# Two-layer hybrid block on one core: when the gathers are queued, and where the expert tables are zeroed

## The chip, the cores and the metric

One core of one Trainium2 chip. The metric is device microseconds of one execution of the whole program. A core has five engines that run their own instruction streams in order: PE (matmul, with its weight loads listed as PEld), DVE, ACT, POOL and SP. SP only issues DMAs here, and POOL issues the indirect ones. All DMAs share 16 DMA engines.

## The reference, cut to what matters

Two layers. Each has adaLN and RMSNorm, one input projection, three kinds of attention, an output projection, and then product-key expert retrieval (PEER), whose last step is what the change touches. There are 512 latent and 256 context tokens (six tiles of 128); layer 1 needs only the four latent tiles.

```python
def peer(h, wq, subkeys, u, v):
    q = (h @ wq).astype(jnp.float32).reshape(t, PEER_HEADS, 2, PEER_KDIM // 2)
    s = jnp.einsum('thpd,hpnd->thpn', q, subkeys.astype(jnp.float32))
    s_top, i_top = lax.top_k(s, PEER_TOPK)
    ...
    best, pos = lax.top_k(cand, PEER_TOPK)
    expert = jnp.take_along_axis(cand_idx, pos, axis=-1)
    gate = jax.nn.softmax(best, axis=-1)
    ...
        a = jax.nn.gelu(jnp.einsum('cd,chkd->chk', hc, u[ec]).astype(jnp.float32), approximate=False)
        w = (gc * a).astype(v.dtype)
        return jnp.einsum('chk,chkd->cd', w, v[ec])
```

Each token picks 8 heads x 16 = 128 of 16384 experts; `u` and `v` are 16384 x 1024 per layer.

## The kernel before, in words

**Dense experts.** The kernel does not gather `v`. It streams all of `v` (128 steps of 128 experts, 512 KB each, L1126) and multiplies it on PE with a matrix of weights per token tile, mostly zeros (`vpass`, L1141). It does this for groups of tiles: (2,3,4) and then (5,0,1) in layer 0, (2,3) and then (1,0) in layer 1. Each 512 KB block of `v` is split into two float16 parts, the high one on ACT (L1127) and the low one on DVE (L1128); PE needs both.

**Activations.** For most tiles ("dense": 2, 3, 4, 5 in layer 0; 2, 3, 1 in layer 1) the product with `u` is also dense: `upass` streams `u` in two halves of 64 steps (L1034, L1054; low parts of the splits on DVE, L144, but on POOL for the first 24 steps, L154), and spills the gelu of it to memory. For the others ("picked": 0 and 1 in layer 0; 0 in layer 1) `gather` fetches the picked rows of `u`: per tile 128 indirect DMAs of 128 rows, 512 KB each, issued by POOL (L946) into a ring of three buffers `r`; DVE multiplies each with the tile's own rows `hg` and sums (L952). That sum goes into the tile `a`, of which there is one buffer, so the second picked tile cannot write it until the first one's values have left.

**Tables.** The weights of a tile other than 2 and 3 go through a table of 8 MB in device memory. `Table.clear` zeroes it (eight pieces of 1 MB by SP, L1257). `Table.put` scatters the values with 128 indirect DMAs per tile, issued by POOL (L1266): for dense tiles the gates (`gs`), for picked tiles the finished weights (`a`). `Table.get` reads it back for `vpass` (L1282). The first group of layer 0 needs table 4, the second one tables 5, 0 and 1; `need` emits what is missing before a group begins.

**What sets the order.** The program is emitted by generators in three lists: `rg` (modulation, routing, picks), `bg` (attention, later the gathers), `sq` (puts). `tick(list, rate)` advances a list by so many items per step of `upass` or `vpass`; the rates per half pass are `RATES` for `bg` and `SRATES` for `sq`. A scheduler then orders the instructions of each engine. `queue_behind` gives a gather or a put an order-only tie behind the latest split `lo_ins`; no engine waits for it on the chip. `zg` holds the clears, ticked in `project` once `ch > 3` and flushed at its end. `routing` and `pick` run beside the first half of `upass`; a pick ends with the indices `ix` and `to` (L913) and 128 short DVE instructions `gjk` (L921). The indices of the picked tiles come last.

The zero tile in `mixers` (L286, L287) is allocated per layer in the pool `nqkv`, filled by POOL, and has no other tie.

Of the kernel before, what the change touches and what calls it, by code (L numbers as in the profile page):

```python
# [8 lines left out]
F32 = mybir.dt.float32  # L9
# [20 lines left out]
BIG = -3.0e38  # L30
ROPE_SCALE = {("d", "q"): 32.0 ** -0.5, ("d", "k"): 1.0, ("r", "q"): 1.0, ("r", "k"): 0.125}
RATE_NA, RATE_DF = 2.7, 1.4
RATES = {0: (0.8, 1.0, 1.5, 1.5, 0.0, 0.0), 1: (0.6, 1.2, 0.4, 0.8, 0.0, 0.0)}
SRATES = {0: (2.0, 2.9, 1.6, 1.8, 4.0, 4.0), 1: (1.5, 1.8, 0.9, 1.2, 4.0, 4.0)}
RRATE = (1.3, 1.05)
AHEAD = 2
GST = 2
# [4 lines left out]
ZC = 2048  # L42
# [5 lines left out]
class Hybrid:  # L48
# [22 lines left out]
    def consts(self):  # L71
        nc, c, tmp = self.nc, self.cst, self.tmp
        dl = tmp.tile([128, 128], F32, name="dl")
        nc.gpsimd.iota(dl, pattern=[[1, 128]], base=0, channel_multiplier=-1,
                       allow_small_or_imprecise_dtypes=True)
        io = tmp.tile([128, 128], F32, name="io")
        nc.gpsimd.iota(io, pattern=[[1, 128]], base=0, channel_multiplier=0,
                       allow_small_or_imprecise_dtypes=True)
        self.idf = c.tile([128, 128], F32, name="idf")
        nc.vector.tensor_scalar(self.idf, dl, 0.0, None, op0=OP.is_equal)  # L80
        self.idh = c.tile([128, 128], F16, name="idh")
        nc.vector.tensor_scalar(self.idh, dl, 0.0, None, op0=OP.is_equal)
        self.iox = c.tile([128, 128], F16, name="iox")
        nc.vector.tensor_copy(self.iox, io)
        self.tok = c.tile([128, 1], F32, name="tok")
        nc.gpsimd.iota(self.tok, pattern=[[0, 1]], base=0, channel_multiplier=1, allow_small_or_imprecise_dtypes=True)
        self.mhalf = c.tile([128, 8], F32, name="mhalf")
        nc.vector.memset(self.mhalf, -0.5)
        self.bcol = c.tile([128, 12, KC], F32, name="bcol")
        nc.gpsimd.dma_start(self.bcol, self.i["b_ada"])  # L90
        self.modT, self.g1, self.g2 = {}, {}, {}
        for l in range(2):
            self.modT[l] = [c.tile([128, KC, 2], F32, name=f"mod{l}_{m}") for m in range(6)]
            for nm, st in (("g1col", self.g1), ("g2col", self.g2)):
                st[l] = c.tile([128, KC], F32, name=f"{nm}{l}")
                nc.gpsimd.dma_start(st[l], self.i[nm][l])
# [173 lines left out]
    def mixers(self, l, last, wes):  # L270
# [11 lines left out]
        with ExitStack() as e:  # L282
            nap = self.pool(e, "nqkv")
            self.naT = nap.tile([128, 4, 2, T], F16, name="naT")
            self.nav = [nap.tile([128, 2, 2, 256], F16, name=f"nav{p}") for p in range(3)]
            self.zero = nap.tile([128, ZC // 4], F32, name="zero")  # L286
            self.nc.gpsimd.memset(self.zero, 0.0)  # L287
            hp = self.pool(e, "hT", 3)
            pp = self.pool(e, "prj", 2)
            ps = self.pool(e, "pps", 2, space=PSUM)  # L290
# [1 line left out]
            if l == 0:  # L292
                spare = lambda t: self.hp2.tile([128, D], F32, name=f"h2T{t}")
                vec = [self.srow(spare(x), x) for x in range(2)]
                n = iter("hl" * 99)
# [68 lines left out]
    def project(self, l, last, hp, pool, ps, ap_, att_es, xs):  # L364
        nc = self.nc
        wv = self.i["w_in"][l].rearrange("(k p) n -> p k n", p=128)

        def load(ch):
            res = []
            for k in range(0, KC, 2):  # L370
# [1 line left out]
                nc.sync.dma_start(w, wv[:, k:k + 2, ch * 256:ch * 256 + 256])  # L372
                h = pool.tile([128, 2, 256], F16, name="wh", bufs=6)
                lo = pool.tile([128, 2, 256], F16, name="wl", bufs=6)
                self.wsplit(h, lo, w)
                res += [(h[:, x], lo[:, x]) for x in range(2)]
            return res

# [645 lines left out]
    def upass(self, l, half, ps, tag, rrate, more=None):  # L1024
        nc = self.nc
# [17 lines left out]
        for jj in range(64):  # L1043
# [22 lines left out]
            if jj % 2:  # L1066
                next(steps, None)
            self.tick(self.rg, rrate)
            self.tick(self.bg, RATES[l][half])
            self.tick(self.sq, SRATES[l][half])  # L1070
        self.drain(steps)

# [161 lines left out]
class Table:  # L1234
# [19 lines left out]
    def clear(self):  # L1254
        o = self.o
        for c in range(0, 128 * 128, ZC):
            self.before.append(o.nc.sync.dma_start(self.view()[:, c:c + ZC].rearrange("i (r n) -> i r n", r=4),  # L1257
                                                  o.zero[:, None].to_broadcast([128, 4, ZC // 4])))
            yield

    def put(self, h, to, values, c, step):
# [93 lines left out]
```

## Time and profile before

| | |
|---|---|
| three runs | 4929.35 us median (4927.22 to 4931.84) |
| profiled execution | 4932.08 us, span 4930.0 us |
| PE, DVE, ACT, POOL busy | 84%, 69%, 40%, 38% |
| mean granted TensorE clock | 0.921 |
| DMA | 971.54 MB, mean 197 GB/s |
| gathers (L946), puts (L1266) | 384, 768 |
| zero pieces (L1257) | 48 of 1 MB |

The stages that the text speaks of lie so: layer 0 projects and attends until about 360 us; retention and the output projection until about 600 us; the first half of `upass` with the routing until about 1190 us; the second half until about 1612 us; the first group of `vpass` until about 2405 us; the second group until about 2920 us. Layer 1 repeats this: projections from about 2945 to 3250 us, `upass` until about 4195 us, `vpass` to the end. Busy time tells how long an engine had an instruction in work; an engine that stands still because its next instruction waits shows as idle, with the name of what ended the wait.

### The profile page before, as it was taken

The numbers are of one execution on the slowest core, as the hardware profiler recorded it, in microseconds if no ns is written. First come the engines' busy times: TensorE is split into PE (matmuls) and PEld (weight loads), VectorE is DVE, ScalarE is ACT, GpSimd is POOL, SyncE is SP. The second block draws the span as 40 slices with busy tenths as digits, with TensorE's granted clock in tenths as the row PEclk, the third lists the DMA queues.
The fourth block names the chain that finished last, engine by engine and source line by source line (L and its number), as shares of the span: only waits on it lengthen the run. The fifth ranks groups of instructions, "written<-read, shape, count | busy, mean of one in ns | idle before, by whom it ended". The sixth has DMA issues, their size and how long they took to land. (4 is left out here: it accounts for less than half of the span.)

```text
span 4930.0 us, 74817 instructions
## 1 busy us (share of the span) xinstructions
PE 4154.8 (84%) x27326; PEld 2287.3 (46%) x27326; DVE 3391.1 (69%) x7913; ACT 1981.4 (40%) x3236; POOL 1877.5 (38%) x1536
## 2 busy tenths in 40 slices
PE   4987888987898889567599999978879888999998
PEld 3664453753444334222244447745546445444443
DVE  7677559889555776566466554574698867987665
ACT  4556353432222334112233336564525322554444
POOL 4224214303777774567500002251213577761000
PEclk8997898998999989878799999978989999999999
DMA  7831343324667887977778863114446678777887
GB/s 250 298 127 35 131 124 100 111 75 129 196 207 214 256 263 224 337 262 262 228 252 269 259 219 102 50 42 135 125 127 190 214 255 267 264 259 253 265 270 238
DMA packets 512322, 971.54 MB, mean 197 GB/s; under 512 B 73824, under 2 KB 295488, under 8 KB 511952
## 3 DMA queue, kind: packets, MB, share of 16 engines
q1 hardware_dynamic: 422464, 759.66, 48.0%
q0 software_dynamic: 80032, 201.86, 12.8%
q10 hardware_dynamic: 9456, 5.24, 0.4%
q8 instruction: 214, 3.51, 0.3%
q14 instruction: 156, 1.28, 0.1%
HBM read 861.77 MB, written 104.78 MB: 196 GB/s over the span
## 5 line engine op out<-in xcount | busy, mean ns | idle before, releaser
L1141 PE MATMUL acc<-hl,gst 128*128 128x512 f16 x7680 | 1761.7, 391 | 231.2 <-ACT gst L140 151.7
L1141 PEld LDWEIGHTS <-gst 128*128 128x128 f16 x7680 | 760.8, 100 | 1201.4 <-issue 179.6
L1054 PEld LDWEIGHTS <-hl 128*128 128x128 f16 x6144 | 613.3, 101 | 726.4 <-DVE hl L144 128.7
L1127 ACT ACTIVATE hl<-s 128x1024 f16<-128x1024 f32 x512 | 538.4, 1053 | 748.0 <-PE acc L1141 393.9
L952 DVE SCALAR_TENSOR_TENSOR r<-r,hg 128x1024 f32<-128x1024 f32 x384 | 468.7, 1224 | 458.1 <-DMA r<-peer_u,ix 457.1
L946 POOL DMA_INDIRECT r<-peer_u,ix x384 | 481.8, 1255 | 665.6 <-DVE r L952 240.0
L1128 DVE TENSOR_TENSOR hl<-s,hl 128x1024 f16<-128x1024 f32 x512 | 625.4, 1222 | 140.8 <-ACT hl L1127 138.7
L1054 PE MATMUL pw<-h2Uh,hl 128*128 128x512 f16 (+1 forms) x2048 | 601.9, 371 | 83.4 <-DVE hl L144 71.0
L1054 PE MATMUL pa<-h2Uh,hl 128*128 128x512 f16 (+1 forms) x2048 | 584.2, 363 | 49.7 <-DVE hl L144 49.4
L1266 POOL DMA_INDIRECT table<-a,to x384 | 494.0, 1286 | 172.4 <-issue 122.3
L1266 POOL DMA_INDIRECT table<-gs,to x384 | 470.1, 1224 | 201.9 <-issue 128.8
L161 POOL TENSOR_TENSOR rstd<-rstd,mhalf 128x1 f32<-128x1 f32 x26 | 14.6, 562 | 1117.2 <-DVE rstd L160 1114.5
L1054 PE MATMUL pw<-h2Ul,hl 128*128 128x512 f16 (+1 forms) x1024 | 379.2, 370 | 0.0
L1054 PE MATMUL pa<-h2Ul,hl 128*128 128x512 f16 (+1 forms) x1024 | 371.7, 363 | 0.0
L169 PE MATMUL pj<-wh,hTl 128*128 128x256 f16 x1072 | 295.8, 276 | 3.0 <-DVE hTl L142 2.5
L167 PE MATMUL pj<-wh,hTh 128*128 128x256 f16 x1072 | 295.8, 276 | 1.2 <-ACT hTh L140 1.2
L168 PE MATMUL pj<-wl,hTh 128*128 128x256 f16 x1072 | 296.0, 276 | 0.0
L144 DVE SCALAR_TENSOR_TENSOR hl<-s,hl 128x1024 f16<-128x1024 f32 x208 | 255.8, 1231 | 19.2 <-ACT hl L140 19.1
L1061 ACT ACTIVATE gst<-pa 128x512 f32<-128x512 f32 (+1 forms) x128 | 69.5, 543 | 486.2 <-PE pa L1054 383.7
L154 POOL TENSOR_TENSOR wl<-wst,wh 128x512 f16<-128x512 f32 x96 | 125.3, 1319 | 287.7 <-ACT wh L153 248.8
L140 ACT ACTIVATE hl<-s 128x1024 f16<-128x1024 f32 x208 | 219.1, 1053 | 11.8 <-DMA s<-ut 10.7
L154 POOL TENSOR_TENSOR hl<-s,hl 128x1024 f16<-128x1024 f32 x48 | 106.3, 2218 | 290.0 <-ACT hl L153 264.5
(292 smaller groups left out, 7000.5 us busy)
## 6 DMA issues: line engine op xcount, KB each, us to landing
s<-peer_v SPq DMA_DIRECT2D x512, 512.0 KB, 4.6
s<-ut SPq DMA_DIRECT2D x256, 512.0 KB, 4.3
table<-zero SPq DMA_DIRECT2D x48, 1024.0 KB, 7.7
wq<-peer_wq SPq DMA_DIRECT2D x128, 256.0 KB, 3.7
spill<-gst SPq DMA_DIRECT2D x112, 256.0 KB, 4.5
wst<-w_in SPq DMA_DIRECT2D x96, 256.0 KB, 3.1
h2Ul<-table SPq DMA_DIRECT2D x192, 128.0 KB, 3.5
h2Uh<-table SPq DMA_DIRECT2D x192, 128.0 KB, 3.4
```

Of the source, the lines that this page charges most:

```text
L144: return nc.vector.scalar_tensor_tensor(lo, src, scale, hi, op0=OP.mult, op1=OP.subtract)
L154: return (lo_eng or nc.gpsimd).tensor_tensor(lo, w, hi, op=OP.subtract)
L167: nc.tensor.matmul(out, ah, bh, start=start, stop=False)
L168: nc.tensor.matmul(out, ah, bl, start=False, stop=False)
L169: nc.tensor.matmul(out, al, bh, start=False, stop=stop)
L946: self.queue_behind(nc.gpsimd.indirect_dma_start(out=r, out_offset=None, in_=self.i["peer_u"], in_offset=bass.IndirectOffsetOnAxis(ap=ix[: ...
L952: nc.vector.scalar_tensor_tensor(r, r, 1.0, h, op0=OP.mult, op1=OP.mult, accum_out=a[:, d // 16, d % 16:d % 16 + 1])
L1054: nc.tensor.matmul(pa[:, c:d], uh[:, x, k], h[:, k, c:d], start=k == 0 and i == 0, stop=k == KC - 1 and i == 2)
L1127: nc.scalar.activation(vh[:, 0], v, AF.Copy)
L1128: self.lo_ins = nc.vector.tensor_tensor(vh[:, 1], v, vh[:, 0], op=OP.subtract)
L1141: nc.tensor.matmul(acc[s][hf], pr[:, w, s, j % 2], vh[:, x, hf * 512:hf * 512 + 512], start=j == 0 and i == 0, stop=j == 127 and i == 2)
L1266: ins = o.nc.gpsimd.indirect_dma_start(out=self.d, out_offset=bass.IndirectOffsetOnAxis(ap=to[:, k, h:h + 1], axis=0), in_=values[:, c + s ...
```

## The change

Three edits in `upass`, `Table.clear`/`project` and the two tables of rates:

```diff
-RATES = {0: (0.8, 1.0, 1.5, 1.5, 0.0, 0.0), 1: (0.6, 1.2, 0.4, 0.8, 0.0, 0.0)}
-SRATES = {0: (2.0, 2.9, 1.6, 1.8, 4.0, 4.0), 1: (1.5, 1.8, 0.9, 1.2, 4.0, 4.0)}
+RATES = {0: (1.0, 1.4, 1.4, 1.4, 0.0, 0.0), 1: (1.0, 1.2, 0.5, 0.9, 0.0, 0.0)}
+SRATES = {0: (3.0, 2.6, 1.6, 1.8, 4.0, 4.0), 1: (2.5, 1.8, 0.9, 1.2, 4.0, 4.0)}
...
+        self.zero = c.tile([128, ZC // 16], F32, name="zero")
+        nc.gpsimd.memset(self.zero, 0.0)
...
-            self.zero = nap.tile([128, ZC // 4], F32, name="zero")
-            self.nc.gpsimd.memset(self.zero, 0.0)
...
-                self.wsplit(h, lo, w)
+                self.lo_ins = self.wsplit(h, lo, w)
...
-            self.tick(self.bg, RATES[l][half])
+            self.tick(self.bg, 0 if self.rg else RATES[l][half])
...
-            self.before.append(o.nc.sync.dma_start(self.view()[:, c:c + ZC].rearrange("i (r n) -> i r n", r=4),
-                                                  o.zero[:, None].to_broadcast([128, 4, ZC // 4])))
+            ins = o.nc.sync.dma_start(self.view()[:, c:c + ZC].rearrange("i (r n) -> i r n", r=16),
+                                      o.zero[:, None].to_broadcast([128, 16, ZC // 16]))
+            o.queue_behind(ins)
+            self.before.append(ins)
```

A piece of zeros is still 1 MB, now read from 512 B of each partition (16 repeats) in place of 2 KB (4 repeats), and tied behind the newest split of a `w_in` block. The zero tile is filled once, at the start. `upass` hands out no gather while `rg` holds routing or picks.

**POOL, end of the first half of `upass` in layer 0.** Before (`table_4` is tile 4's table, `r<-peer_u,ix` a gather):

```order
L154 TENSOR_TENSOR hl<-s_9374,hl 128x1024
L1266 DMA table_4_102<-gs,to 2097152x1 x68
L946 DMA r<-peer_u,ix 128x1024
L1266 DMA table_4_102<-gs,to 2097152x1 x2
L946 DMA r<-peer_u,ix 128x1024
L1266 DMA table_4_102<-gs,to 2097152x1 x2
L946 DMA r<-peer_u,ix 128x1024
L1266 DMA table_4_102<-gs,to 2097152x1 x4
```

And now (line numbers of this part are two higher):

```order
L156 TENSOR_TENSOR hl<-s_9374,hl 128x1024
L1268 DMA table_4_104<-gs,to 2097152x1 x128
L1268 DMA table_5_105<-gs,to 2097152x1 x5
L946 DMA r<-peer_u,ix 128x1024 x2
L1268 DMA table_5_105<-gs,to 2097152x1 x3
L946 DMA r<-peer_u,ix 128x1024
L1268 DMA table_5_105<-gs,to 2097152x1 x3
```

The first gather stood behind 68 puts and now stands behind 133. Counting gathers and puts together, the 11th gather was the 103rd of them and the 4th is now the 143rd; the 81st was the 360th and is the 363rd, the 128th the 456th and the 466th, the 256th the 736th and the 752nd. In both orders the last put of tile 0 is the 515th and the last of layer 0 the 768th.

**SP, first group of `vpass` in layer 0** (`s<-peer_v` is a block of `v`, `table_0_26984` a table of layer 1). Before:

```order
L1126 DMA s_20957<-peer_v 128x1024
L1126 DMA s_20993<-peer_v 128x1024
L1282 DMA h2Ul<-table_4_102 128x256
L1086 DMA h2Ul<-spill_6783 128x2x384
L1257 DMA table_0_26984<-zero 128x4x512
L1126 DMA s_21024<-peer_v 128x1024
L1126 DMA s_21059<-peer_v 128x1024
L1257 DMA table_0_26984<-zero 128x4x512
```

Now these pieces stand in layer 1's projections, from the 26th of its 48 loads of `w_in` (`wst`) to the 37th:

```order
L372 DMA wst<-w_in 128x2x256
L1257 DMA table_0_26984<-zero 128x16x128 x4
L524 DMA bias<-bias 128x768 x2
L372 DMA wst<-w_in 128x2x256 x2
L524 DMA bias<-bias 128x768
L372 DMA wst<-w_in 128x2x256
L524 DMA bias<-bias 128x768
L372 DMA wst<-w_in 128x2x256
L1257 DMA table_0_26984<-zero 128x16x128 x4
L1257 DMA table_1_26985<-zero 128x16x128
L372 DMA wst<-w_in 128x2x256 x3
```

All 16 pieces of layer 1 moved so, behind some 600 other DMAs. The 32 of layer 0 stood between the 6th and the 33rd load of `w_in` and now stand from the 26th on, in runs of up to five.

**DVE, first group of `vpass` in layer 0, where the second picked tile's products begin** (`r,a<-r,hg`). Before, behind the 72nd split of `v`:

```order
L1128 TENSOR_TENSOR hl<-s_21193,hl 128x1024
L1128 TENSOR_TENSOR hl<-s_21223,hl 128x1024
L1096 TENSOR_TENSOR h2Ul<-P,h2Ul 128x512
L1099 TENSOR_TENSOR h2Ul<-h2Ul 128x256
L952 SCALAR_TENSOR_TENSOR r,a<-r,hg 128x1024 x3
L142 TENSOR_TENSOR gst<-h2Uh,gst 128x768
```

Now, behind the 59th:

```order
L1128 TENSOR_TENSOR hl<-s_20742,hl 128x1024
L1212 TENSOR_TENSOR oj<-iox,sT 128x512
L1099 TENSOR_TENSOR h2Ul<-h2Ul 128x256
L952 SCALAR_TENSOR_TENSOR r,a<-r,hg 128x1024 x3
L1128 TENSOR_TENSOR hl<-s_20798,hl 128x1024
```

The first picked tile's last product moved from behind the 40th split of `v` to behind the 32nd, the second one's last from behind the 127th to behind the 124th. At the last split of `upass` 68 products were through and now 81; by the 72nd split of `v` 128 were and now 170. Ahead of the 70th of `upass`'s 128 splits stood 8 products and now none. In layer 1, 20 of the 128 products stood ahead of the end of `upass`'s first half and now 2; `vpass` holds 50 of them in place of 33, 6 of the 17 more within its first 64 steps, and the last stands behind its 82nd split in place of the 70th.

## Rows read from the trace of the kernel before

**Rows 1.** Windows of layer 0: us; busy us (instructions) by engine; clock, DMA share, GB/s.

```profile
918.00:1119.00 201.00, 183.82 (x1789) 121.30 (x1787) 173.59 (x833) 76.98 (x146) 0.46 (x1) 0.96 0.30 92
1234.00:1612.00 378.00, 337.69 (x1890) 156.38 (x1888) 208.22 (x308) 91.11 (x122) 280.20 (x232) 0.95 0.70 207
1612.00:1844.00 232.00, 192.96 (x1094) 88.19 (x1093) 177.59 (x293) 76.56 (x132) 170.60 (x134) 0.91 0.80 261
1844.00:1966.00 122.00, 120.63 (x724) 57.49 (x723) 78.19 (x112) 48.49 (x77) 57.76 (x50) 1.00 0.70 219
1966.00:2386.00 420.00, 277.85 (x1011) 107.93 (x1008) 263.31 (x395) 81.42 (x91) 279.52 (x221) 0.83 0.85 287
2386.00:2441.00 55.00, 11.06 (x36) 4.10 (x36) 15.85 (x21) 13.44 (x20) 40.94 (x38) 0.61 0.53 169
```

**Rows 2.** Timeline of POOL: start, duration, instruction, idle before it and releaser.

```profile
1119.69 1.05 POOL L946 DMA_INDIRECT r<-peer_u,ix  x1 [201.23 <-DVE ix L913]
1234.51 4.05 POOL L946 DMA_INDIRECT r<-peer_u,ix  x1 [28.33 <-DVE r L952]
```

**Rows 3.** Waits of DVE for gathers from 1234 to 1612 us: total, times, longest.

```profile
DVE r L952 <- DMA r<-peer_u,ix: 168.7, 38, 8.7
```

**Rows 4.** Windows of line L952 on DVE alone; each product shows as two instructions.

```profile
1234.00:1612.00 378.00, 75.62 (x124) 0.95 0.70 207
1966.00:2200.00 234.00, 90.78 (x149) 0.80 0.88 304
2200.00:2386.00 186.00, 63.82 (x104) 0.86 0.80 265
```

**Rows 5.** Windows of line L1128 (splits of `v`) on DVE alone.

```profile
1844.00:1966.00 122.00, 37.90 (x31) 1.00 0.70 219
1966.00:2200.00 234.00, 33.21 (x27) 0.80 0.88 304
```

**Rows 6.** Window of POOL alone, the last part of the gathers of layer 0.

```profile
2200.00:2386.00 186.00, 144.68 (x115) 0.86 0.80 265
```

**Rows 7.** Timeline of POOL around the zero tile of layer 1.

```profile
1926.14 0.52 POOL L287 MEMSET zero<- 128x512 f32 x1 [27.90 <-DVE gst L142]
1954.42 0.96 POOL L1266 DMA_INDIRECT table<-a,to  x1 [0.31 <-issue]
1970.52 1.72 POOL L946 DMA_INDIRECT r<-peer_u,ix  x1 [15.14 <-DVE r L952]
```

**Rows 8.** Timelines of POOL and PE where the second group begins: last put, first matmuls.

```profile
2435.88 0.96 POOL L1266 DMA_INDIRECT table<-a,to  x1 [0.30 <-issue]
2441.19 29.08 PE L1141 MATMUL acc<-hl,gst 128*128 128x512 f16 x124 [36.61 <-ACT gst L140]
```

**Rows 9.** Line L1257: issue time in ns, first and last start; us from issue to landing.

```profile
L1257 SPq DMA_DIRECT2D table<-zero x48: 417/460/1689, 61.7 to 2067.3; - x48
DMA to landing us min/median/max: 5.9/7.7/11.7
```

**Rows 10.** SP's queue from 600 to 800, then 60 to 260 us: packets, MB, share of 16 engines.

```profile
q1 hardware_dynamic: 27474, 24.84, 41.3%
...
q1 hardware_dynamic: 29975, 57.69, 85.2%
```

**Rows 11.** Windows: layer 0's projections; then layer 1's, its routing, and first group of `vpass`.

```profile
60.00:360.00 300.00, 255.41 (x2433) 199.44 (x2433) 213.17 (x406) 169.24 (x328) 74.98 (x58) 0.96 0.70 234
...
3080.00:3180.00 100.00, 90.43 (x919) 70.70 (x917) 52.99 (x89) 60.83 (x111) 22.38 (x20) 1.00 0.18 54
3640.00:3875.00 235.00, 182.80 (x1546) 122.19 (x1544) 210.62 (x869) 93.76 (x198) 79.53 (x66) 0.90 0.53 163
...
4195.00:4400.00 205.00, 197.75 (x1346) 97.05 (x1347) 192.91 (x271) 109.25 (x170) 140.46 (x99) 0.97 0.79 263
```

**Rows 12.** Windows of line L952 on DVE alone, layer 1: routing, first part of `vpass`.

```profile
3640.00:3875.00 235.00, 25.74 (x42) 0.90 0.53 163
...
4195.00:4400.00 205.00, 37.61 (x63) 0.97 0.79 263
```

## The prediction

> **What bounds the kernel now.** I took the windows by stage first, then POOL's timeline, then the waits. In layer 0 from 1234 to 1844 us no engine shows as full; PE comes nearest, with 83% to 89% [rows 1]. But each of POOL's indirect DMAs is followed by a gap of 0.30 us in which nothing is waited for [rows 7, 8]. From 1234 to 1612 us POOL issues 232 of them: 280.2 us busy and 232 x 0.30 = 70 us of gaps are 350 of 378 us. So POOL's queue is the limit there, at 378 / 232 = 1.63 us each, and from 1612 to 1844 us at 232 / 134 = 1.73. It reaches PE through DVE: DVE works in order, stands 168.7 us for gathers to land [rows 3], and the splits that PE needs are behind these products. The clock follows: 0.95 and 0.91, against 1.00 (2.4 GHz) from 1844 to 1966 us, where no product is in the way [rows 1].
>
> Why is POOL late? From 918 to 1119 us it issued nothing [rows 1]: its next instruction was the first gather, which waited 201.23 us for the indices, with puts behind it whose values were there. It stood again, 28.33 us until 1234 us, for a buffer that a product had to free [rows 2].
>
> Two more places. From 1844 to 1966 us DVE's order holds no product, and 31 steps of `vpass` take 122 us, 3.94 each [rows 5], with POOL held 27.90 us by the zero tile's memset [rows 7]. Then the second tile's 128 gathers are crammed into the rest of the group: 75 products in 234 us, 3.12 each, then 52 in 186 us, 3.58 each [rows 4], while a step of `vpass` costs 234 / 27 = 8.7 us [rows 5]. PE is 66% busy from 1966 to 2386 us [rows 1]. Layer 1's zeros run into the beginning of this, until 2067 us [rows 9]. The group ends late, and the next one waits for the last put: issued at 2435.88, first matmul at 2441.19, after 36.61 us of idle PE [rows 8].
>
> **The gathers of layer 0, step by step.** Positions are those of the orders shown; times per item are those above.
>
> (1) Of the products ahead of `upass`'s 70th split 8 go, 8 x 1.22 = 10 us (75.62 us for 62, [rows 4]). The indices come from the same work as before, so the first gather still starts near 1119 us. The first new product then ends near 1227 us, where before it was 1234 when POOL went on.
>
> (2) At that point POOL has done 142 items instead of 102, because 65 more puts fit into the 201 us in which it stood: at 0.96 and the gap of 0.30 each [rows 8] they need 82. From the 143rd to the 363rd item, the 81st gather: 220 x 1.63 = 359, so 1586 us. That is the end of `upass` (1612 before).
>
> (3) To the 128th gather: 466 - 363 = 103 items x 1.73 = 178, so 1764 us at the 32nd step of `vpass`. At 3.94 a step PE would need 126, so POOL still decides.
>
> (4) No products for 27 steps, to the 59th: 27 x 3.94 = 106, so 1870 us, 96 before the 1966 us of now. The 49 puts that must be out of the way need 62, and the memset is gone.
>
> (5) Products 129 to 170, by the 72nd step: 42 of them. Their price is 3.12 with layer 1's zeros beside them. About ten of those pieces fell into that window; at 3.1 us of transfer each (below) they take at most 31 of 234 us, which leaves 2.7 as the lower bound. I take 3.0: 126, so 1996 us.
>
> (6) Items 567 to 752: 185 x 1.62 (186 us for 115, [rows 6]) = 300, so 2296 us. The remaining 56 steps of PE would need 221.
>
> (7) Sixteen puts at 1.26 and 5 us to the first matmul: 25, so 2321 us against 2441: **120 us gained**. Before, POOL issued 38 items from 2386 to 2441 us [rows 1].
>
> Bounds. POOL at busy time plus gap alone (1.51, 1.57 and 1.56 us) and 2.7 for (5) give 2254, 187 gained. With 1.73 in (2), 3.58 in (5) and 3.58 for each of the 86 products of (6), and the old 55 us in (7), it is 2405, 36 gained.
>
> **Layer 1.** Its picks and routing lose 18 products. From 3640 to 3875 us they take 25.74 us of a DVE that is 90% busy [rows 11, 12]. Bounds 0 and 23; I take 15. They come back in `vpass`: 6 in the first 64 steps, where DVE is busy 192.9 of 205 us [rows 11] and has 31 already [rows 12], 11 behind. Bounds 0 and -21 (17 x 1.22); I take -5, since only the 6 meet a full DVE. The table is needed by the second group, 46 steps after the last product, so `need` has nothing to wait for.
>
> **The zeros.** A piece becomes 2048 packets of 512 B instead of 512 of 2 KB. Two windows of SP's queue price this: 27474 packets and 24.84 MB take 41.3% of 16 engines for 200 us, 29975 and 57.69 MB take 85.2% [rows 10]. Solved for a part per packet and one per byte: 10.2 ns and 42.0 us per MB of one engine. So 512 B cost 31.7 ns and 2 KB 96.2 ns, and a piece 4.1 us instead of 3.1 of all engines. The Trainium skill speaks against this edit too (*DMA: Bandwidth & Descriptors*, Why small descriptors are slow (HBM only)): about 3 cycles per packet beside 32-byte beats, which would be 19 beats for 512 B and 67 for 2 KB, 13% more in all. By that estimate a piece would go from 3.1 to 3.5 us; the rows' 33% is the dearer of the two.
>
> The work that hides it: in layer 1 the DMA share is 0.18 at the new place, so 82 of 100 us are free for 16 x 4.1 = 66 [rows 11]. In layer 0, 32 x 4.1 = 131 us go into the last 190 or so of the projections instead of being spread over them; the whole stretch is at 0.70 [rows 11]. What is queued behind a piece on SP are loads of `w_in`, `bias` and the modulation weights; in a run of four they stand 16 us longer, and DVE and ACT wait for those, then PE. Bounds: +10 (the first half gets free of zeros) and -60 (four such runs fully felt); I take -5, because with the pieces between its loads PE still was 255 of 300 us busy [rows 11]. The fill at the start costs under 1 us.
>
> **Sum.** 120 + 15 - 5 - 5 = 125. The profiled execution took 4932 us, 2.7 above the median of the runs; 4932 - 125 = 4807, or on the runs' scale **4805 us**.
>
> **Rivals.**
> - *Landing limits, not POOL's queue.* Then the head start in (2) is worth nothing: the 128th product comes at 1830 instead of near 1838, the hole ends at 1936, and (5), (6) at 3.12 and 3.58 give 2375, (7) 2401: 40 gained, 45 with the rest, 4885. For it: DVE waits for landing [rows 3]. Against: it waits so at 6.1 us a product (378 / 62), and gathers land at 3.12 when POOL sends them faster [rows 4]. Chance 0.12.
> - *More.* Without the zeros the crammed stretch runs at the lower bounds: 187 and the 5 of the rest, 4737. For it: DMA at 0.88 there [rows 5]. Chance 0.09.
> - *Slower: the zeros become the bound of the projections.* If every piece is felt, 48 x 4.1 = 197 us against the 130 of the other terms: 67 slower, 4996. It decides from 130 / 48 = 2.7 us felt per piece. For it: a piece lands after 7.7 us [rows 9], and the runs of up to five stand ahead of loads. Against: DMA shares of 0.18 and 0.70 [rows 11]. By the page's estimate it would be 48 x 3.5 = 168 and 4967. Chance 0.04.
> - *No difference, or the change doesn't do what it says:* the tie is order-only, so pieces might not follow the splits, and another wait could hold the second group. But SP works in order and the pieces stand behind loads that wait for buffers, and the wait that ended last there was a put [rows 8]. Chance 0.04.
>
> **How the numbers follow.** The forecast keeps 0.71. Its own range is 4745 to 4870 (gains of 60 to 185, from the bounds, short of all of them falling on one side). To leave out no more than 2 in 10 the range takes in the first two rivals: **4735 to 4885**. About 0.2% (10 us) is what a measurement of this kernel can tell from no change. Faster: forecast, the first two rivals, 0.92. Same 0.04, slower 0.04.
>
> **What would show it.** In the new profile POOL should issue puts from 920 to about 1005 us and wait some 110, not 201, for the indices; `upass` should end near 1590, products of the second tile start near 1870, the first group's last put come near 2316, and the first matmul of the second group near 2321. No zeros should be issued between 1900 and 2100 us. PE's busy share from the projections of both layers should be unchanged within 5%. I am wrong if the second half of `upass` takes as long as before with the same wait for landing, if the hole in DVE's order ends later than 1930 us, or if waits for `w_in` or `bias` appear in the projections.

## The result, and the profile after

| | before | change |
|---|---|---|
| median, us (4 runs each, one chip) | 4928.28 (4915.01 to 4931.84) | 4876.76 (4868.07 to 4882.17) |
| ratio, 95% interval | 1 | 0.9899 [0.9875, 0.9922] |
| profiled span, us | 4930.0 | 4873.3 |
| mean granted clock | 0.921 | 0.929 |
| busy PE, DVE, ACT, POOL | 84%, 69%, 40%, 38% | 85%, 70%, 41%, 38% |
| packets of all DMAs | 512322 | 586050 |

The change is faster by 51.5 us between medians, 56.7 between the two profiles. The forecast was 124. The sign was right, the size was more than twice too large.

Windows of the changed kernel by stage, cut at the same events as [rows 1]:

```profile
918.00:1133.00 215.00, 197.75 (x1997) 133.56 (x1997) 185.01 (x879) 85.09 (x161) 74.26 (x72) 0.96 0.34 98
1243.00:1611.00 368.00, 333.41 (x1886) 155.20 (x1884) 228.42 (x342) 90.06 (x122) 268.61 (x226) 0.96 0.78 237
1611.00:1796.00 185.00, 150.14 (x885) 69.75 (x882) 139.68 (x227) 59.40 (x102) 131.14 (x102) 0.93 0.78 255
1796.00:1906.00 110.00, 107.26 (x670) 51.48 (x669) 74.44 (x115) 46.52 (x80) 56.78 (x47) 0.98 0.58 182
1906.00:2332.00 426.00, 303.31 (x1267) 125.56 (x1266) 290.81 (x434) 97.33 (x116) 300.09 (x237) 0.89 0.82 276
2332.00:2381.00 49.00, 17.22 (x75) 7.49 (x75) 18.71 (x22) 16.79 (x24) 23.02 (x22) 0.72 0.70 218
```

POOL now works from 918 to 1133 us (74.26 us busy, 0.46 before), the third window is 185 us long instead of 232, and the stretch with the second tile's products is 426 us at clock 0.89 instead of 420 at 0.83. The last window, from the last product to just after the second group's first matmul, is almost as long as it was (49 against 55 us; by the stamps below 46 against 47).

POOL's timeline of the changed kernel, first and fourth gather (as [rows 2]), and DVE's waits for gathers from 1243 to 1611 us (as [rows 3]):

```profile
1133.24 1.05 POOL L946 DMA_INDIRECT r<-peer_u,ix  x1 [109.46 <-DVE ix L913]
...
1245.58 0.97 POOL L946 DMA_INDIRECT r<-peer_u,ix  x1 [100.39 <-DVE r L952]
```

```profile
DVE r L952 <- DMA r<-peer_u,ix: 133.2, 44, 7.8
```

The wait for the indices fell from 201.23 to 109.46 us, as forecast (some 110). But the first gather comes 13.6 us later than before. POOL then stands another 100.39 us for a buffer that the first product must free. The puts next in its queue are those of table 5, and DVE's rows for the gates of the two dense tiles from 700 to 1000 us end at 907 us:

```profile
L921 DVE SCALAR_TENSOR_TENSOR gjk<-ef,sgate x256: 337/352/2208, 806.0 to 907.2; 128x128 bf16<-128x128 f32 x128
```

So their values were there, and at 1.26 us each some 80 puts would have fitted into this wait (an estimate from the 0.96 us and the gap of 0.30 of [rows 8]). The forecast had this wait in step (1) and did not ask for its use; no run moved puts ahead of that gather.

The forecast's own stamps against the trace (ends of products, but the start of the 129th, from the rows of L952; starts of matmuls from those of L1054 and L1141; us):

| | before | forecast | change | late by | of it new |
|---|---|---|---|---|---|
| first matmul of `upass` | 610.9 | 611 + some of 5 | 623.8 | 13 | 13 |
| (1) first new product ends | (1234) | 1227 | 1245 | 18 | 5 |
| (2) 81st product | 1666 | 1586 | 1611 | 25 | 7 |
| (3) 128th product | 1838 | 1764 | 1798 | 34 | 9 |
| (4) products go on | 1969 | 1870 | 1906 | 36 | 2 |
| (5) 170th product | 2100 | 1996 | 2019 | 23 | -13 |
| (6) 256th product | 2394 | 2296 | 2333 | 37 | 14 |
| (7) second group's first matmul | 2441 | 2321 | 2379 | 58 | 21 |

So 62 us are won by the start of the second group, not 120. Layer 1 adds nothing: its projections lose 3, the stretch up to `vpass` wins 19, and `vpass` loses 21 (from the last split of `w_in` and the first of `v`).

The seam between the groups. SP's waits from 2340 to 2385 us, then SP's, PE's and POOL's timelines of the changed kernel:

```profile
SPq L372 <- POOL wl L156: 17.9, 3, 15.9
```

```profile
2344.84 0.57 SPq L227 DMA_DIRECT2D hl<-vec  x1
2361.38 0.37 SPq L372 DMA_DIRECT2D wst<-w_in  x1
...
2370.96 0.42 SPq L237 DMA_DIRECT2D s<-mid  x1
...
2373.60 0.33 SPq L1126 DMA_DIRECT2D s<-peer_v  x1
```

```profile
2378.80 1.01 PE L1141 MATMUL acc<-hl,gst 128*128 128x512 f16 x2 [29.37 <-ACT hl L1127]
```

```profile
2359.21 0.96 POOL L1268 DMA_INDIRECT table<-a,to  x1 [0.30 <-issue]
2360.18 3.38 POOL L156 TENSOR_TENSOR wl<-wst,wh 128x512 f16<-128x512 f32 x3
```

Before, the first matmul followed the last put by 5.3 us [rows 8]; now by 19.6, and PE waits for ACT's split of `v`, not for the table. SP stands from 2345.4 to 2361.4 us at a load of layer 1's `w_in` that the scheduler had brought forward. Its buffer is freed by a split on POOL, and that split is queued behind the last twelve puts. On SP, behind this load, stand the first group's residual loads (`s<-mid`) and, behind those, the second group's first `v`.

The zeros. Line L1257 of the changed kernel (as [rows 9]), and two windows of layer 0's projections, of the change and then of the kernel before:

```profile
L1257 SPq DMA_DIRECT2D table<-zero x48: 414/2914/4406, 206.3 to 3101.1; - x48
```

```profile
60.00:200.00 140.00, 113.64 (x993) 88.83 (x994) 87.78 (x174) 75.11 (x137) 37.34 (x28) 0.90 0.41 126
200.00:360.00 160.00, 139.72 (x1364) 105.66 (x1362) 104.71 (x199) 85.34 (x176) 37.13 (x26) 0.97 0.80 237
```

```profile
60.00:200.00 140.00, 117.80 (x1074) 93.36 (x1075) 92.28 (x177) 81.53 (x146) 37.90 (x30) 0.94 0.86 288
200.00:360.00 160.00, 137.61 (x1361) 106.07 (x1358) 120.89 (x230) 87.70 (x184) 37.08 (x28) 0.98 0.56 186
```

A piece now holds SP for 2.9 us in the median, 0.46 before; none is issued between 1900 and 2100 us any more. PE is as busy as the forecast asked (253.4 of 300 us against 255.4), and yet the stage ends 13 us later. Most of the loss lies before the first piece is issued at 206.3 us: from 60 to 200 us PE gets through 993 matmuls instead of 1074, with the DMA engines at 0.41. At 117.80 / 1074 us each the 81 are some 9 of the 13 us. From 200 to 360 us it does as many as before (1364 against 1361), and the rest is lost after that.

### The profile page after: what moved, and what is told of

Same layout as the page of the kernel before. It is cut to its first block, busy times and chain, and to the rows that moved or that the text cites. A ratio compares the mean times of both kernels' runs of the same rounds, so it can differ in the third digit from the quotient of the medians.

```text
span 4873.3 us, 74858 instructions
## 1 busy us (share of the span) xinstructions
PE 4123.4 (85%) x27326; PEld 2278.3 (47%) x27326; DVE 3396.4 (70%) x7913; ACT 1979.8 (41%) x3236; POOL 1846.4 (38%) x1535
## 2 busy tenths in 40 slices
DMA packets 586050, 971.54 MB, mean 199 GB/s; under 512 B 73824, under 2 KB 393792, under 8 KB 585680
## 5 line engine op out<-in xcount | busy, mean ns | idle before, releaser
L1141 PE MATMUL acc<-hl,gst 128*128 128x512 f16 x7680 | 1733.0, 386 | 202.8 <-DVE hl L1128 75.2
L1141 PEld LDWEIGHTS <-gst 128*128 128x128 f16 x7680 | 754.3, 99 | 1151.2 <-issue 178.2
L1054 PEld LDWEIGHTS <-hl 128*128 128x128 f16 x6144 | 609.2, 101 | 724.5 <-DVE hl L146 136.8
L952 DVE SCALAR_TENSOR_TENSOR r<-r,hg 128x1024 f32<-128x1024 f32 x384 | 468.8, 1224 | 382.6 <-DMA r<-peer_u,ix 382.0
L1128 DVE TENSOR_TENSOR hl<-s,hl 128x1024 f16<-128x1024 f32 x512 | 626.3, 1224 | 143.7 <-ACT hl L1127 141.4
L1054 PE MATMUL pw<-h2Uh,hl 128*128 128x512 f16 (+1 forms) x2048 | 598.1, 369 | 78.2 <-DVE hl L146 69.5
L1054 PE MATMUL pa<-h2Uh,hl 128*128 128x512 f16 (+1 forms) x2048 | 580.0, 361 | 59.5 <-DVE hl L146 56.5
L1268 POOL DMA_INDIRECT table<-gs,to x384 | 443.0, 1154 | 278.6 <-issue 135.7
L163 POOL TENSOR_TENSOR rstd<-rstd,mhalf 128x1 f32<-128x1 f32 x26 | 15.5, 595 | 1138.6 <-DVE rstd L162 1136.0
L1054 PE MATMUL pw<-h2Ul,hl 128*128 128x512 f16 (+1 forms) x1024 | 376.8, 368 | 0.0
L1054 PE MATMUL pa<-h2Ul,hl 128*128 128x512 f16 (+1 forms) x1024 | 369.1, 360 | 0.0
L921 DVE SCALAR_TENSOR_TENSOR gjk<-ef,sgate 128x128 bf16<-128x128 f32 x768 | 217.3, 375 | 0.0
```

What stands on the lines that cost most here:

```text
L921: nc.vector.scalar_tensor_tensor(jk, e, e[:, k:k + 1], g, op0=OP.is_equal, op1=OP.mult, accum_out=o[:, k:k + 1])
L952: nc.vector.scalar_tensor_tensor(r, r, 1.0, h, op0=OP.mult, op1=OP.mult, accum_out=a[:, d // 16, d % 16:d % 16 + 1])
L1054: nc.tensor.matmul(pa[:, c:d], uh[:, x, k], h[:, k, c:d], start=k == 0 and i == 0, stop=k == KC - 1 and i == 2)
L1128: self.lo_ins = nc.vector.tensor_tensor(vh[:, 1], v, vh[:, 0], op=OP.subtract)
L1141: nc.tensor.matmul(acc[s][hf], pr[:, w, s, j % 2], vh[:, x, hf * 512:hf * 512 + 512], start=j == 0 and i == 0, stop=j == 127 and i == 2)
L1268: ins = o.nc.gpsimd.indirect_dma_start(out=self.d, out_offset=bass.IndirectOffsetOnAxis(ap=to[:, k, h:h + 1], axis=0), in_=values[:, c + s ...
```

## The experiments

Medians and ratios stand against runs of before on the same chip; the 12 kernels ran on three chips, four on each. Counts of products and splits are those of the trace's rows. Line numbers are those of each kernel.

**Parts of the change.** `zeros_only` keeps the zero edits and puts `RATES`, `SRATES` and the gate back; `gate_rates` is the reverse:

```diff
 zeros_only, against the change
-            self.tick(self.bg, 0 if self.rg else RATES[l][half])
+            self.tick(self.bg, RATES[l][half])
 gate_rates, against the kernel before
-            self.tick(self.bg, RATES[l][half])
+            self.tick(self.bg, 0 if self.rg else RATES[l][half])
```

> The zero edits of the change alone (512 B source, ties behind the splits of w_in), with the old rates and no gate on the gathers. Theory A (what the profile after suggests): a piece of 2048 packets holds SP's queue for about 2.9 us, so the projections of layer 0 end about 14 us later and those of layer 1 about 3 us; against that the zero tile's memset and 16 pieces leave the first group of vpass. Sum between 20 us slower and 10 us faster, ratio 0.998 to 1.004. Theory B (the recorded forecast): 5 us lost in the projections, and less crowding in vpass of layer 0 gives up to 31 us back: 0 to 26 us faster, ratio 0.995 to 1.000, with the first matmul of layer 0's upass not more than 5 us late.

> The gate on the gathers and the new rates alone; the tables are zeroed as before. Theory A: the order of the gathers carries the whole gain of the change and more, since the projections lose nothing: 51 + 14 + 3 = 68 us faster, ratio 0.986, with upass of layer 0 beginning as before (first matmul 611 us). Rival: taking the zeros and the memset out of layer 0's vpass is what lets the second tile's products run faster, and without it 10 to 30 us of that are lost: 20 to 60 us faster, ratio 0.988 to 0.996.

`zeros_only`: 4913.56 against 4909.22, ratio 1.0000 [0.9990, 1.0009]. The first matmul of `upass` comes at 620.5 us, 11 later than in the kernel before on a chip of this study (609.3). That is theory A's loss in size, and the sum is nought because something comes back. `gate_rates`: 4879.25, ratio 0.9930 [0.9915, 0.9945], first matmul at 609.8. It gains 30 us, so theory A's 68 is refuted and the rival stands: from the 129th to the 256th product `gate_rates` needs 450.6 us, and `zeros_2k` below, on the same chip and with layer 1's zeros gone from there, 435.2. Between `ctl_before` below and `zeros_only`, which share the old order of the gathers, it is 425.1 against 410.3. About 15 us are given back there and about 11 taken in layer 0's projections; the two halves of the zero edit cancel.

**Controls.** The change and the kernel before, unedited, on one chip:

> The changed kernel once more, beside the runs of before on the same chip, since the four runs above share a chip whose runs of before (4909 us) were 19 us faster than those beside which the change was first timed. If the gain is a property of the program: ratio 0.990, about 50 us. If it depends on the chip (on what the throttle grants before and after): like the two kernels above that hold the whole order of the gathers, ratio 0.992 to 0.993, about 35 us.

> The kernel before, for its profile on this chip, so that stages can be compared without the difference of chips: within 0.3 per cent of the other runs of before here. In the profile the first matmul of layer 0's upass should come near 610 us, and the second tile's last product near 2385 us if this chip is only faster where the clock is granted higher.

`ctl_after`: 4883.32 against 4922.95, ratio 0.9923 [0.9907, 0.9940], 40 us. `ctl_before`: 4924.17 in one run, first matmul of `upass` at 609.3, 256th product ended at 2385.7. The gain is some 40 to 50 us; the intervals of the two ratios overlap, so whether it depends on the chip is not settled. The growing lag of the stamps is there too: 622.1, 1611.6, 1799.2, 1906.9, 2346.0 us for the first matmul and the products 81, 128, 129 and 256 (taken as in the table). This profile is that of the slowest of its six runs, 10 us above their median, with the same order of instructions as the change's above; it is within 2 us of that up to the 129th product and 13 later at the 256th.

**What of the zeros costs layer 0.** `zeros_2k` keeps every piece at its new place and makes it 512 packets again (its zero tile, 2 KB a partition, is once more filled per layer, behind an early split of `w_in`); `zeros_l1` also takes the tie away in layer 0, so that the pieces return to where they stood before, and leaves it in layer 1:

```diff
 zeros_2k (parts of lines)
-rearrange("i (r n) -> i r n", r=16), o.zero[:, None].to_broadcast([128, 16, ZC // 16])
+rearrange("i (r n) -> i r n", r=4), o.zero[:, None].to_broadcast([128, 4, ZC // 4])
 zeros_l1, besides
-                self.lo_ins = self.wsplit(h, lo, w)
+                ins = self.wsplit(h, lo, w)
+                if l:
+                    self.lo_ins = ins
```

> The changed kernel with every piece at its new place in SP's order, but read from 2 KB of each partition (512 packets) again; the zero tile is filled behind a split of w_in. Theory A (the number of packets costs SP's queue its time): issue back from 2.9 us to about 0.46 us a piece, the projections of layer 0 back to their old end (first matmul of upass at 611 instead of 624 us, DVE's 21st split of u at 1011 instead of 1024 us), 3 us more in layer 1: 13 to 17 us faster than the change, ratio 0.986 to 0.987. Rival (the place costs, not the packets: bytes that are squeezed into 190 us delay the loads of w_in): the first matmul of upass stays 10 us or more late, ratio 0.989 to 0.991.

> The changed kernel with 2 KB pieces, and with layer 0's pieces untied, so that they stand between the 6th and the 33rd load of w_in as before; layer 1's keep their new place. Theory A (the late, dense place costs layer 0's projections about 10 us whatever the packets, and the old place costs nothing): first matmul of layer 0's upass at 610 to 612 us, and 8 to 12 us faster than the change. Rival (the head start is lost again in the stretch that POOL's queue paces, as part of it was between the 20th and the 60th split of u): first matmul near 611 us, but the second group begins less than 5 us earlier, and the time is within 5 us of the change.

Line of the pieces in `zeros_2k` and its first window of the projections, then both windows of `zeros_l1`:

```profile
L1257 SPq DMA_DIRECT2D table<-zero x48: 414/505/2478, 205.6 to 3097.4; - x48
...
60.00:200.00 140.00, 113.58 (x998) 89.10 (x999) 88.87 (x177) 74.94 (x137) 37.46 (x28) 0.91 0.41 126
```

```profile
60.00:200.00 140.00, 118.94 (x1077) 93.62 (x1077) 93.52 (x181) 81.85 (x146) 37.49 (x30) 0.98 0.85 289
200.00:360.00 160.00, 138.47 (x1369) 107.54 (x1369) 119.72 (x228) 87.37 (x184) 38.22 (x28) 0.98 0.56 186
```

`zeros_2k`: 4877.46, ratio 0.9927 [0.9913, 0.9941]. The issue is back at 0.5 us, but the first matmul still comes at 621.7 us. My theory that the packets did it is refuted: against 623.8 in the change they are worth 2 us at most, and `zeros_only`, with 2048 packets a piece on the same chip, had 620.5. `zeros_l1`: 4858.56, ratio 0.9877 [0.9854, 0.9899], first matmul at 609.1 us, PE back at 1077 matmuls in the first window. It is 25 us faster than `ctl_after` on the same chip, twice what I had expected: the 13 us at the first matmul are 18 at the 81st product, 20 at the 128th and 25 at the second group. So it is the place and what it does to the order of the projections, not the size of the packets. Part of it shows in SP's timeline of the change and of the kernel before:

```profile
84.36 7.63 SPq L188 DMA_DIRECT2D h2T<-w_ada  x2
93.77 1.14 SPq L524 DMA_DIRECT2D bias<-bias  x2
98.71 1.49 SPq L372 DMA_DIRECT2D wst<-w_in  x2
```

```profile
85.45 0.34 SPq L186 DMA_DIRECT2D h2T<-w_ada  x1
85.85 0.42 SPq L1257 DMA_DIRECT2D table<-zero  x1
89.92 1.55 SPq L524 DMA_DIRECT2D bias<-bias  x2
94.54 2.60 SPq L372 DMA_DIRECT2D wst<-w_in  x3
```

Without the early pieces the scheduler set other loads in their stead: two loads of modulation weights (`w_ada`) in a row, which with their waits hold SP for 7.6 us, and behind them `w_in` 4 us later. Waits of DVE for `w_ada` and of ACT for `w_in` before the first piece is issued (60 to 206 us), then that of DVE beside the first 22 pieces (206 to 360 us), in the change and in the kernel before:

```profile
DVE wjk L195 <- DMA h2T<-w_ada: 36.2, 13, 7.4
ACT wst L154 <- DMA wst<-w_in: 21.0, 10, 4.3
...
DVE wjk L195 <- DMA h2T<-w_ada: 5.4, 4, 3.1
```

```profile
DVE wjk L193 <- DMA h2T<-w_ada: 22.8, 11, 7.5
ACT wst L152 <- DMA wst<-w_in: 13.9, 7, 4.0
...
DVE wjk L193 <- DMA h2T<-w_ada: 10.7, 7, 3.5
```

The longer waits lie wholly ahead of the first piece (35.4 and 18.3 us in `zeros_2k`, 21.8 and 13.2 in `zeros_l1`); beside the pieces they are shorter than before (ACT's 6.0 us against 7.3). So some 9 of the 13 us are lost at the place that the pieces left, where the DMA engines had less to do than before. `zeros_l1` undoes both places at once; what loses the last 4 us, after 360 us, is not shown.

**The seam.** `seam` ties layer 1's first loads of `w_in` behind the second group's 65th split of `v`. `seam2` also ties the table loads of the second group's first two pairs of steps behind the first group's last add:

```diff
 seam
-                nc.sync.dma_start(w, wv[:, k:k + 2, ch * 256:ch * 256 + 256])
+                ld = nc.sync.dma_start(w, wv[:, k:k + 2, ch * 256:ch * 256 + 256])
+                if l and ch == 0:
+                    self.queue_behind(ld, self.late)
 seam2, besides, in Table.get
+        of = o.seam if j <= 2 and not o.last else None
...
+        if of is not None:
+            o.queue_behind(ins, of)
```

> The changed kernel with one more order-only tie: layer 1's first four loads of w_in may not stand ahead of the 65th split of v of layer 0's second group, so that no load that waits for a split on POOL stands ahead of the second group's first loads of v on SP. Theory A (that load is what keeps SP from 2345 to 2361 us): the first matmul of the second group follows the last put by about 5 us instead of 19.6, near 2365 us; 10 to 15 us faster than the change, ratio 0.987 to 0.988, less up to 5 us if layer 1 begins later. Rival (the tables' last puts and the loads of them decide anyway): first matmul at 2375 to 2380 us, ratio 0.989 to 0.991.

> The kernel seam with one more tie: in layer 0's second group, the loads of the three tables for its first two pairs of steps may not stand ahead of the first group's last add, so that SP, which waits in those loads for the last put, no longer holds back the first group's last residual load and the second group's first load of v. Theory A (a chain through SP: get, residual load, add, buffer s, load of v, ACT's split): the first matmul of the second group follows the last put by 7 to 10 us instead of 15.5 (seam) or 22 (the change), so 10 to 15 us faster than the change and 6 to 8 faster than seam. Rival (the last tables have to land, be multiplied and split anyway): still 15 us behind the last put, and within 3 us of seam.

Timelines of POOL's last put and PE's first matmul in `seam` with SP's longest wait from 2350 to 2385 us, then of PE's in `seam2`, whose last put is issued at 2367.38:

```profile
2366.98 0.95 POOL L1273 DMA_INDIRECT table<-a,to  x1 [0.30 <-issue]
...
2381.20 1.01 PE L1146 MATMUL acc<-hl,gst 128*128 128x512 f16 x2 [21.18 <-ACT hl L1130]
...
SPq L1289 <- DMA table<-a,to: 12.1, 1, 12.1
```

```profile
2375.31 10.06 PE L1146 MATMUL acc<-hl,gst 128*128 128x512 f16 x35 [13.25 <-ACT gst L142]
```

`seam`: 4867.56, ratio 0.9906 [0.9891, 0.9922], 10 us faster than `zeros_2k` on the same chip. The first matmul follows the last put by 14.2 us instead of 19.6, where I expected 5 (`seam2`'s expectation gives 15.5 and 22 for the first two; the timelines have 14.2 and 19.6): SP now stands 12.1 us at a table load that waits for the put, with the residual load behind it. `seam2` takes that away too: 7.9 us, and PE waits for the table's weights (`gst`) again, as before. Its ratio is 0.9897 [0.9876, 0.9918]; against `seam`, on another chip, the times do not tell the two apart. Both waits are shown in the timeline; the gain of the second step is only seen there. `gate_rates`, with the old zeros, has 18.9 us from put to matmul, so this wait comes with the order of the gathers and not with the zeros.

**POOL's queue or landing.** `puts_half` leaves out every second put, so its tables hold half of the weights:

```diff
         for k in range(16):
+            if k % 2 == 0:
+                yield
+                continue
...
```

> The changed kernel without every second put (the picks 0, 2, 4 and so on of each head never reach the tables, so the tables hold half of the weights); gathers, products, splits and matmuls stand in the same order. Theory A (the queue of POOL paces layer 0 from the first product on): from the first to the 81st product POOL has 149 items instead of 220, 243 us at 1.63, so that PE's own pace decides and the stretch falls from 366 us to 300 to 320; the second tile's products need 330 to 350 us instead of 426; the second group begins 150 to 220 us earlier. Rival (the landing of the gathers decides, 6.1 us a product here and 3.1 to 3.6 there whatever stands between them): both stretches within 15 us of the change's.

Its windows from the first to the 81st product and from the 129th to the 256th, DVE's wait for gathers in the first, and POOL's for buffers in the second, here and in the change (1906 to 2332 us):

```profile
1243.00:1552.00 309.00, 309.00 (x1835) 147.22 (x1833) 227.23 (x337) 88.54 (x119) 181.77 (x154) 1.00 0.86 281
1829.00:2219.00 390.00, 298.05 (x1269) 125.70 (x1268) 290.45 (x433) 98.71 (x117) 242.29 (x181) 0.89 0.88 301
...
DVE r L952 <- DMA r<-peer_u,ix: 12.6, 13, 2.9
...
POOL r L946 <- DVE r L952: 165.3, 62, 68.5
...
POOL r L946 <- DVE r L952: 85.0, 44, 35.9
```

One run, 4708.12 us. In `upass` the 81st product needs 310 us instead of 366, PE is never idle, the clock is 1.00 (2.4 GHz), and DVE waits 12.6 us for gathers instead of 133.2. So POOL's queue was the limit of that stretch, and the rival of landing falls there. The run takes the puts' packets off the DMA engines together with their issues off POOL; it does not separate the two, but the DMA share did not fall (0.86 against 0.78). In `vpass` it is otherwise: 390 us instead of 426, where I expected 330 to 350, and the second group begins 117 us earlier, where I expected 150 to 220. With 76 of its 280 items gone, POOL's waits for a buffer that a product must free grow to 97 us, from 49 in the change (without the longest wait of each, 68.5 and 35.9 us). That points to the ring of three buffers, from issue over landing to product, at 3.07 us a product; no run changed the ring, so this much is argued.

**Layer 1.** `l1_old` has the old rates and no gate in layer 1 (of the tables of rates, its entries alone):

```diff
-RATES 1: (1.0, 1.2, 0.5, 0.9, 0.0, 0.0), SRATES 1: (2.5, 1.8, 0.9, 1.2, 4.0, 4.0)
+RATES 1: (0.6, 1.2, 0.4, 0.8, 0.0, 0.0), SRATES 1: (1.5, 1.8, 0.9, 1.2, 4.0, 4.0)
-            self.tick(self.bg, 0 if self.rg else RATES[l][half])
+            self.tick(self.bg, 0 if self.rg and not l else RATES[l][half])
```

> The changed kernel, but layer 1 with its old rates and without the gate, so that 20 of its 128 products stand beside the routing again and 33 in vpass. Theory A (the 18 products only change their place: 16 to 20 us gained in the routing, 20 lost in vpass): within 6 us of the change, with layer 1's first v split 13 to 20 us later than in the change, counted from the end of layer 0, and the last v split within 6 us. Theory B (the recorded forecast: 15 gained, 5 lost): 10 us slower than the change.

The first 97 splits of layer 1's `vpass` in `l1_old`, and the same 97 in `ctl_after` on the same chip:

```profile
4141.00:4414.00 273.00, 264.70 (x1654) 127.28 (x1655) 241.50 (x325) 143.88 (x210) 183.60 (x132) 0.98 0.80 262
```

```profile
4126.00:4422.00 296.00, 269.29 (x1679) 127.77 (x1680) 262.35 (x364) 144.98 (x214) 168.69 (x125) 0.97 0.83 274
```

4881.99 us against `ctl_after`'s 4883.32, ratio 0.9918 [0.9898, 0.9937]. The gate takes 20.9 us of DVE's work out of the routing and puts it into this stretch, which gets 23 us longer. In the time theory A holds: layer 1 gains nothing by the gate. Two of its signs missed in these profiles: counted from the end of layer 0, the first split of `v` comes 11 us later in `l1_old` (13 to 20 expected) and the last one 16 earlier (within 6 expected). Between `best` and `best_l1` below the two are 25 us later and 2 later.

**Together.** `best` is `zeros_l1` with the ties of `seam2`; `best_l1` has `l1_old`'s edit besides:

```diff
 best: the lines of zeros_l1 and seam2, so
+                if l:
+                    self.lo_ins = ins
+        of = o.seam if j <= 2 and not o.last else None
 best_l1, besides
+            self.tick(self.bg, 0 if self.rg and not l else RATES[l][half])
```

> zeros_l1 and seam2 together: layer 0's zeros at their old place with 512 packets a piece, layer 1's in its projections, and the ties at the seam. If the two add: 25 us from the zeros and 10 to 15 from the seam, ratio 0.984 to 0.986, 35 to 40 us faster than the change. If the earlier group only waits elsewhere (POOL's last puts): like zeros_l1 alone, 0.988.

> best with layer 1's old rates and no gate there. By theory A on layer 1 (its 18 products only change their place) it is within 6 us of best; by the recorded forecast 10 us slower; if the loss in vpass is the larger of the two, 5 to 10 us faster.

`best`: 4854.90 against 4912.53, ratio 0.9884 [0.9867, 0.9902]; `best_l1`: 4842.25, ratio 0.9854 [0.9831, 0.9877], which is 70 us faster than the kernel before and the fastest that does the whole work. In `best`'s profile the second group begins at 2351.7 us with 7.8 us from the last put, as the two parts together promised. But that profile is of the fastest of its five runs, which lie at 4842.67 to 4858.19; their median is 10 us below `seam2` on the same chip and not the 25 between `zeros_l1` and `ctl_after`: in time the two do not plainly add. `best_l1` is 12.6 us below `best`, more than the 5 to 10 I had allowed, with intervals that overlap; in the two profiles the routing's 22.5 and `vpass`'s 22.8 us cancel, so whether the gate in layer 1 costs anything is left open.

## Why the prediction was right in kind and wrong in size

**What bounds the kernel: right, and shown for `upass`.** POOL stood idle for the indices (201 us, now 109), its queue paced the stretch from 1243 to 1800 us, and more puts in the idle time ended that stretch earlier (1798 against 1838 us). `puts_half` shows the queue as the limit there.

**Step (1) to (6): nearly right in length, late in start.** From the first product to the 256th the forecast had 1069 us, the trace has 1088. (2) came out at 1.66 us an item instead of 1.63, (3) at 1.81 instead of 1.73; what made an item dearer is not settled. (5) ran at the lower bound I had named (113 us for 42 products, 2.7 each, since layer 1's zeros were gone; with them in place `gate_rates` needs 128), (6) 14 us over. For (5) and (6) together I had 426 us, and 427 it was. That is luck: `ctl_after` needs 439 with the same order, and I priced (6) by POOL's items, while `puts_half` shows that they are not the whole of what paces it.

**A step that failed: the zeros, "I take -5, because with the pieces between its loads PE still was 255 of 300 us busy".** They took 13.6 us in layer 0 and 2.9 in layer 1, and without layer 0's tie the second group begins 25 us earlier (`zeros_l1` against `ctl_after`). My price was one of packets and transfer (4.1 us a piece instead of 3.1). From 200 to 360 us 22 pieces and the loads beside them took 79.2% of 16 engines in the change and 70.0% in `zeros_2k`, though the change moved 2% fewer bytes: 14.7 us for 22 pieces, 0.7 us more each (0.8 by the 80.8% of `zeros_only`, at the same bytes as `zeros_2k`). Mine from the rows was 1.0. An estimate from what the Trainium skill states (*DMA: Bandwidth & Descriptors*, Why small descriptors are slow (HBM only)) would be 0.4. The price of a piece does not decide the time, as `zeros_2k` shows. What did was the order: the pieces that stood early had kept other loads apart, and some 9 of the 13 us were lost there. I had asked only what is queued behind them at the new place, not what moves up at the old one. PE's busy share, my sign for this step, did not show it; the number of matmuls in the first window did, and so did longer waits for `w_in`, one of my signs of being wrong (28.3 us from 60 to 400 us, 22.7 before).

**Step (7), "Sixteen puts at 1.26 and 5 us to the first matmul: 25".** It measured 46: 2.7 until the first of those puts, 23.6 from the first to the last with two of layer 1's splits of `w_in` in between, and 19.6 to the matmul. The 5 us of before [rows 8] were taken at a seam where the last put was issued 31 us after PE's last matmul of the first group, so that the rest of the seam was hidden. Now it is issued 10 us after it, and SP's order became the wait. `seam` and `seam2` show both links of it.

**Layer 1, "I take -5, since only the 6 meet a full DVE".** The routing gave 19 us (forecast 15; 13 between the two controls), and `vpass` took 21, the whole lower bound: the 11 products that I had left out of account fell where PE waits for DVE's splits as well, 7 waits of 11.3 us in all from 4310 to 4408 us against one of 0.8 beside the same splits before (4384 to 4468 us).

**The sum.** 125 forecast, 56.7 between the profiles: 11 by the zeros' own delay, 24 in steps (1) to (6), 21 at the seam, 12 in layer 1. Part of the 24 is the zeros' delay again, and open is why that delay grows: from 13 us at the start of `upass` to 21 at the 129th product and 25 at the second group (`ctl_after` against `zeros_l1`), from 9 to 21 and 24 (`seam2` against `best`), with the same order of DVE's and POOL's instructions in between. Behind the 129th product single executions of one order differ by as much as 12 us (427 and 439), so the last figures are uncertain. The time, 4877, lies outside my own range of 4745 to 4870; the stated one holds it by the room made for a rival. The rival of landing (4885) gave nearly the right time for another reason: `upass` did not wait for landing. That the zeros bound the projections was a rival of mine too, but with its price on each piece, and from 200 to 360 us 22 pieces cost PE nothing.

## What to carry to other kernels

Where a change takes instructions out of an in-order queue, look at both ends: what now stands behind them at the new place, and what moves up at the old one; the scheduler here filled the gap with loads that wait. A tail that was measured while another wait covered it ("5 us from the last put to the first matmul") is no price for the day when that wait is gone: list everything that the next stage needs, by queue, and see which comes second. Work that is moved from one stage to another is gained only if the receiving stage has room on the same engine; where DVE was 94% busy, 17 products cost their whole 21 us.

## What the runs showed of the hardware that was not expected

A DMA of 2048 packets of 512 B holds SP's queue for 2.9 us in the median, one of 512 packets of 2 KB with the same bytes for 0.5 us (48 of each). Although that is some 115 us of SP's time, the effect on the end of layer 0's projections was 2 us at most (first matmul of `upass` at 623.8 and 621.7 us). And with half of the puts gone PE ran 309 us without a gap at a granted clock of 1.00 (2.4 GHz), while in `vpass`, 71% busy with all puts and 76% with half, it was granted 0.89 on the mean in both.
